# Last layer's feed-forward products by Strassen's scheme: seven products of quarters, the second product's left operands by way of DRAM

## The chip, the cores and the metric

The kernel runs on one core of a Trainium2 chip. The metric is the device time of one execution, in microseconds (us); a lower time is better.

## The reference

Three different layers follow one another on one sequence of 1024 rows with 1024 features (all float32): a hybrid layer with gated linear attention, a layer with an mLSTM and windowed attention, and a layer with a gated delta net and neighbourhood attention. The change lies in the end of the third. Its mixer's result `mix` is projected, added to x and normalized, and then comes the feed-forward part with 4096 hidden features:

```python
D_FF_3 = 4 * D_MODEL            # 4096, D_MODEL = 1024
...
mix = jnp.einsum('bte,ed->btd', jnp.concatenate([o_gdn, o_na], axis=-1), w_out[l])
x = layer_norm(DEEPNORM_ALPHA * x + mix, ln1_g[l], ln1_b[l])
ff = jnp.square(jax.nn.relu(jnp.einsum('btd,df->btf', x, w1[l]) + b1[l]))
ff = jnp.einsum('btf,fd->btd', ff, w2[l]) + b2[l]
x = layer_norm(DEEPNORM_ALPHA * x + ff, ln2_g[l], ln2_b[l])
```

## The kernel before

Engines: TensorE (PE) multiplies, VectorE (DVE), ScalarE (ACT) and GpSimd (POOL) do the elementwise work, SyncE (SP) issues the DMAs in one queue, in order. Operations are written into the program in one order per engine; each engine takes its own in order and waits at semaphores. Names of tiles come with a running number.

Every float32 operand of a product is split into a high and a low part of a shorter float32 (`fp32r`): hi is a cast by ACT, lo = x - hi a subtraction by DVE (`part`, and `piece`, L67 and L68, for weights). A product is then three matmuls, hi·hi, hi·lo and lo·hi (L123 to L125 in `tm`, L139 to L141 in `fm`). One matmul here is 128 by 128 against 512 columns.

Weights arrive in 512 KB pieces: `piece` loads into a tile `wraw` (a pool of two buffers, `rawpool`), casts, subtracts and frees it; the parts lie in `w` (six buffers). So only two such loads are under way or held at a time. The left operand x, turned so that features lie on partitions, lies in the four tiles `Thi`, `Tlo` of `new_T` (pool `tpool`, four buffers of 16 KB per partition).

The tail of the third layer has three parts:

- `out_late` finishes the output projection for eight blocks m of 128 rows: it loads the partial sum into `acc[m]`, adds two products on DVE (L335), normalizes (`ln_rows`, L248 to L255: ACT Square and Identity, DVE multiply L254, POOL add L255) and turns the rows into `T4` by eight transposes (`put_T`, L106).
- `up(g)` makes 256 hidden features of all 1024 rows: 2 halves x 2 x 8 x 3 = 96 matmuls; ACT takes Relu and Square, and a cast and a DVE subtraction split the result into `hh`, `hl` in SBUF.
- `down` multiplies them with the rows of the second weight and adds to `acc` on DVE (L1973): 8 row blocks x 2 x 2 x 3 = 96 matmuls.

With 16 groups g these are 16 x 192 = 3072 matmuls. `up(g + 1)` is written ahead of `down(g)`. At the last group the final normalization (`ln_halves`, L263 to L270) follows each row block and its two halves go out. GpSimd adds the bias b2 to each `acc[m]` once (L1962).

## Time and profile before

| what | value |
|---|---|
| three runs | 3817.88, 3821.74, 3827.13 us (median 3821.74) |
| the profiled execution's own time | 3819.98 us |
| its span in the trace | 3818.3 us |
| mean granted clock | 0.98 of full speed |

The span is what the trace covers from the first to the last instruction; the profiled execution's time lies 1.7 us above it. All times below in the rows are us from the start of the span; durations of single instructions are in ns where a view says mean ns. Matmuls are pipelined: the trace gives one about 0.39 us, but they start every 0.23 us, so their spacing and not their duration counts.

### The profile page before, as it was taken

The numbers are of one execution on the slowest core, as the hardware profiler recorded it, in microseconds if no ns is written. First come the engines' busy times: TensorE is split into PE (matmuls) and PEld (weight loads), VectorE is DVE, ScalarE is ACT, GpSimd is POOL, SyncE is SP. The second block draws the span as 40 slices with busy tenths as digits, with TensorE's granted clock in tenths as the row PEclk, the third lists the DMA queues.
The fourth block names the chain that finished last, engine by engine and source line by source line (L and its number), as shares of the span: only waits on it lengthen the run. The fifth ranks groups of instructions, "written<-read, shape, count | busy, mean of one in ns | idle before, by whom it ended". The sixth has DMA issues, their size and how long they took to land.

```text
span 3818.3 us, 49447 instructions
## 1 busy us (share of the span) xinstructions
PE 3680.5 (96%) x18856; PEld 3067.6 (80%) x18856; DVE 1901.2 (50%) x4073; ACT 1288.7 (34%) x2767; POOL 588.9 (15%) x637
## 2 busy tenths in 40 slices
...
GB/s 128 50 61 72 45 56 80 132 186 54 34 51 84 128 173 56 34 56 45 56 45 55 108 128 129 103 92 134 109 146 131 128 100 50 45 45 55 45 49 51
DMA packets 182556, 317.48 MB, mean 83 GB/s; under 512 B 33296, under 2 KB 112400, under 8 KB 182320
## 3 DMA queue, kind: packets, MB, share of 16 engines
...
q14 instruction: 87, 0.71, 0.1%
...
## 4 chain that ended last, share of the span: by engine, by line
PE 83%; DVE 8%; DMA 4%; ACT 3%; issue 1%; POOL 1%; SPq 1%; DVEq 0%; ACTq 0%; POOLq 0%
PE mm L123 11%; PE mm L125 11%; PE mm L124 11%; PE mm L139 6%; PE mm L141 6%; PE mm L140 6%; PE mx L139 4%; PE mx L141 4%; PE mx L140 4%; PE mx L123 3%; PE mx L124 3%; PE mx L125 3%; PE pt L106 1%; DVE ip L1523 1%; PE mx L1772 1%
## 5 line engine op out<-in xcount | busy, mean ns | idle before, releaser
L123 PE MATMUL mm<-w,Thi 128*128 128x512 f32 (+1 forms) x1920 | 685.5, 357 | 14.4 <-ACT Thi L111 3.1
L125 PE MATMUL mm<-w,Tlo 128*128 128x512 f32 (+1 forms) x1920 | 676.5, 353 | 0.0
L124 PE MATMUL mm<-w,Thi 128*128 128x512 f32 (+1 forms) x1920 | 674.6, 351 | 1.0 <-DVE w L68 1.0
L139 PE MATMUL mm<-Thi,w 128*128 128x512 f32 (+1 forms) x1240 | 496.6, 401 | 10.0 <-DVE qo L513 4.9
L140 PE MATMUL mm<-Tlo,w 128*128 128x512 f32 (+1 forms) x1240 | 491.1, 396 | 0.0
L141 PE MATMUL mm<-Thi,w 128*128 128x512 f32 (+1 forms) x1240 | 490.2, 396 | 0.0
L67 ACT CAST w<-wraw 128x1024 fp32r<-128x1024 f32 (+2 forms) x253 | 261.0, 1034 | 646.3 <-PE mx L125 423.5
L123 PEld LDWEIGHTS mm<-w,Thi 128*128 128x128 f32 x1920 | 365.2, 190 | 66.1 <-DVE acc L335 5.1
L125 PEld LDWEIGHTS mm<-w,Tlo 128*128 128x128 f32 x1920 | 365.0, 190 | 49.9 <-issue 3.5
L124 PEld LDWEIGHTS mm<-w,Thi 128*128 128x128 f32 x1920 | 365.4, 190 | 47.5 <-issue 2.5
L68 DVE TENSOR_TENSOR w<-wraw,w 128x1024 fp32r<-128x1024 f32 (+2 forms) x210 | 262.1, 1250 | 236.0 <-ACT w L67 230.5
L57 POOL TENSOR_TENSOR st<-st,expo 128x1 f32<-128x1 f32 x48 | 47.6, 991 | 1569.2 <-DVE st L264 1446.4
L139 PEld LDWEIGHTS mm<-Thi,w 128*128 128x128 f32 (+1 forms) x1240 | 235.0, 189 | 64.7 <-issue 9.4
L139 PE MATMUL mx<-Thi,w 128*128 128x512 f32 (+1 forms) x760 | 285.3, 375 | 0.5 <-DVE anm L1047 0.2
L140 PE MATMUL mx<-Tlo,w 128*128 128x512 f32 (+1 forms) x760 | 284.2, 374 | 0.2 <-DVE Tlo L112 0.2
L141 PE MATMUL mx<-Thi,w 128*128 128x512 f32 (+1 forms) x760 | 284.1, 374 | 0.0
L141 PEld LDWEIGHTS mm<-Thi,w 128*128 128x128 f32 (+1 forms) x1240 | 234.7, 189 | 52.6 <-issue 2.6
L140 PEld LDWEIGHTS mm<-Tlo,w 128*128 128x128 f32 (+1 forms) x1240 | 235.0, 189 | 50.4 <-issue 2.5
L123 PE MATMUL mm<-w,hh 128*128 128x512 f32 x432 | 170.9, 396 | 0.2 <-DVE acc L1208 0.2
L124 PE MATMUL mx<-w,hh 128*128 128x512 f32 x432 | 170.9, 396 | 0.0
L125 PE MATMUL mx<-w,hl 128*128 128x512 f32 x432 | 170.8, 395 | 0.0
L123 PE MATMUL mx<-w,hh 128*128 128x512 f32 x432 | 170.7, 395 | 0.0
...
## 6 DMA issues: line engine op xcount, KB each, us to landing
...
```

What stands on the lines that cost most here:

```text
L57: self.nc.gpsimd.tensor_tensor(ap, ap, self.expo[:parts, :n], op=ALU.pow)
L67: nc.scalar.copy(w[:, 1], raw)
L68: (nc.gpsimd if self.pool_lo else nc.vector).tensor_sub(w[:, 0], raw, w[:, 1].bitcast(F32))
L106: nc.tensor.transpose(pt[:, k], src[:, (j + k) * P:(j + k + 1) * P], self.idn)
L123: nc.tensor.matmul(ps, hi[:, k, cs], wh, start=start and x == 0, stop=False)
L124: nc.tensor.matmul(ps, hi[:, k, cs], wl, start=False, stop=False)
L125: nc.tensor.matmul(ps, lo[:, k, cs], wh, start=False, stop=stop and x == K - 1)
L139: nc.tensor.matmul(ps, wh, hi[:, k0 + k], start=k == 0, stop=False)
L140: nc.tensor.matmul(ps, wh, lo[:, k0 + k], start=False, stop=False)
L141: nc.tensor.matmul(ps, wl, hi[:, k0 + k], start=False, stop=k == K - 1)
L1523: nc.vector.tensor_mul(v, X[:, c0:r, c0:c0 + n].rearrange("p j c -> p c j"), row[:, None, c0:r].to_broadcast([P, n, r - c0]))
L1772: nc.tensor.matmul(ps[:, :nk], qv, kv, start=True, stop=True)
```

## The change

Both products of the feed-forward part are written as two by two quarters and done by seven products of quarters in place of eight (Winograd's form of Strassen's scheme). For the up product x has the quarters A11 to A22 (512 rows by 512 features) and each unit u of 256 hidden features has four weight quarters a, b, cc, d of 512 by 128; the sums of quarters of x are S1 to S4, those of the weights are made in place by `combine` on GpSimd. Products accumulate in PSUM and ACT copies intermediate sums aside (`snap`). For the down product the left quarters are the hidden features: their sums are made as each unit is finished (`left_parts`), and all seven left operands of each unit are written to DRAM (`hid`, 256 KB each), from where `left` loads them again, two units in one 512 KB load, and splits them into hi and lo. x itself goes to DRAM (`xs_scr`) behind the first normalization and comes back into `acc` ahead of the down product. A unit has 7 x 12 = 84 matmuls in the up product; the down product has 4 groups of four units, each with 7 products of 48 matmuls.

The diff, cut where "..." stands (the removed code of the feed-forward part is printed above):

```diff
@@ -321,11 +321,16 @@
-def out_late(c, w, scale, T, ks, y, g, b, acc, T4, junk):
+def out_late(c, w, scale, T, ks, y, g, b, acc, T4, junk=None, each=None):
     nc = c.nc
     W = [rows_of(c, w[j], ks, scale) for j in range(2)]
+    if each is not None:
+        new, acc = acc, {}
     for m in range(NT):
+        if each is not None:
+            acc[m] = new(m)
...
-        ln_rows(c, acc[m], sm, g, b, junk)
-        c.put_T(T4, m, acc[m])
+        if each is None:
+            ln_rows(c, acc[m], sm, g, b, junk)
+            c.put_T(T4, m, acc[m])
+        else:
+            jk = c.rawpool.tile([P, 2, 512], F32, name="wraw", tag="wraw")
+            ln_rows(c, acc[m], sm, g, b, jk.rearrange("p a b -> p (a b)"))
+            each(m, acc[m])
...
+LEFT = ("A11", "A12", "A22", "S1", "S2", "S3", "S4")
+OF = {1: "A11", 2: "A12", 3: "S4", 4: "A22", 5: "S1", 6: "S2", 7: "S3"}
+class Quarters:
+    def __init__(self, c, T, pool, spool):
+        self.c, self.T, self.spool = c, T, spool
+        self.S = {n: [pool.tile([P, 4, 512], F32R, name=f"{n}{x}") for x in "hl"] for n in ("S2", "S3", "S4")}
+        self.kept = {}
...
+    def put(self, n, x, src):
+        c = self.c
+        pt = c.ps_tr.tile([P, 4, P], F32, name="pt", tag="tr")
+        for k in range(4):
+            c.nc.tensor.transpose(pt[:, k], src[:, k * P:(k + 1) * P], c.idn)
+        hi, lo = self.get(n)
+        cs = slice(x * P, (x + 1) * P)
+        c.part(hi[:, :, cs], lo[:, :, cs], pt)
+    def take(self, m, x):
+        nc = self.c.nc
+        lo, hi = slice(0, 512), slice(512, D)
+        if m < 4:
+            self.kept[m] = x
+            self.put("A11", m, x[:, lo])
+            self.put("A12", m, x[:, hi])
+            return
+        y = self.kept.pop(m - 4)
+        s1, s3 = (self.spool.tile([P, 512], F32, name="s", tag="s", bufs=3) for _ in range(2))
+        nc.vector.tensor_add(s1, x[:, lo], x[:, hi])
+        nc.gpsimd.tensor_sub(s3, y[:, lo], x[:, lo])
+        nc.vector.tensor_sub(y[:, lo], s1, y[:, lo])
+        nc.vector.tensor_sub(y[:, hi], y[:, hi], y[:, lo])
+        for n, src in (("A22", x[:, hi]), ("S1", s1), ("S2", y[:, lo]), ("S3", s3), ("S4", y[:, hi])):
+            self.put(n, m - 4, src)
+def combine(nc, a, b, cc, d):
+    nc.gpsimd.tensor_sub(b, d, b)
+    nc.gpsimd.tensor_add(a, b, a)
+    yield
+    nc.gpsimd.tensor_sub(b, cc, a)
+    nc.gpsimd.tensor_sub(a, d, a)
+    yield
+def wino_up(c, src, units, Q, sink):
+    def split(raw, n):
+        w = c.wpool.tile([P, 2, 4, n], F32R, name="w", tag="w", bufs=NW)
+        nc.scalar.copy(w[:, 1], raw)
+        nc.vector.tensor_sub(w[:, 0], raw, w[:, 1].bitcast(F32))
+        return w
+    def prep(u):
+        r1, r2 = (c.rawpool.tile([P, 4, 256], F32, name="wraw", tag="wraw") for _ in range(2))
+        nc.sync.dma_start(r1, src(u)[:, 0:4])
+        nc.sync.dma_start(r2, src(u)[:, 4:8])
+        f, g = slice(0, P), slice(P, 2 * P)
+        steps = combine(nc, r1[:, :, f], r1[:, :, g], r2[:, :, f], r2[:, :, g])
+        w1 = split(r1[:, :, f], P)
+        next(steps)
+        w67 = split(r1, 2 * P)
+        next(steps)
+        w54 = split(r1, 2 * P)
+        w23 = split(r2, 2 * P)
+        return {1: (w1, f), 6: (w67, f), 7: (w67, g), 5: (w54, f), 4: (w54, g), 2: (w23, f), 3: (w23, g)}
...
+    def snap(ps):
+        t = Q.spool.tile([P, 512], F32, name="snap", tag="h")
+        nc.scalar.copy(t, ps)
+        return t
+    W = {0: prep(0)}
+    X = {0: c.mm_ps()}
+    product(1, W[0], X[0], True)
+    c11 = snap(X[0])
+    for u in range(units):
+        w, x = W.pop(u), X.pop(u)
+        if u + 1 < units:
+            W[u + 1] = prep(u + 1)
+        last = u == units - 1
+        y, z = c.mx_ps(), c.mx_ps()
+        if last:
+            product(2, w, y, True)
+        else:
+            product(5, w, z, True)
+        product(6, w, x, False)
+        u2 = snap(x)
+        if not last:
+            product(2, w, y, True)
+        C = {"C11": (y, c11)}
+        product(7, w, x, False)
+        u3 = snap(x)
+        if last:
+            product(5, w, z, True)
+        else:
+            X[u + 1] = c.mm_ps()
+            product(1, W[u + 1], X[u + 1], True)
+            c11 = snap(X[u + 1])
+        C["C22"] = (z, u3)
+        sink(u, C)
+        product(4, w, x, False)
+        C["C21"] = (x, None)
+        sink(u, C)
+        product(3, w, z, False)
+        C["C12"] = (z, u2)
+        sink(u, C)
+def wino_down(c, src, hid, groups, acc, pool, evict):
+    def left(n, u0, u1):
+        t = c.tpool.tile([P, KT, 512], F32R, name="Ahl", tag="T")
+        for u in range(u0, u1, 2):
+            k = min(2, u1 - u)
+            raw = c.rawpool.tile([P, 2, 512], F32, name="wraw", tag="wraw")[:, :k]
+            nc.sync.dma_start(raw, hid[LEFT.index(OF[n]), u:u + k].rearrange("u p n -> p u n"))
+            hi, lo = t[:, u - u0:u - u0 + k], t[:, 4 + u - u0:4 + u - u0 + k]
+            nc.scalar.copy(hi, raw)
+            nc.vector.tensor_sub(lo, raw, hi.bitcast(F32))
+        return t
+    def right(u0, u1):
+        parts = []
+        for x, u in enumerate(range(u0, u1, 2)):
+            k = min(2, u1 - u)
+            q = []
+            for n, (j, o) in (("d", (1, 1)), ("b", (1, 0)), ("a", (0, 0)), ("c", (0, 1))):
+                t = pool.tile([P, 2, 512], F32, name=f"r{n}{x}", tag=f"r{n}{x}", bufs=1)[:, :k]
+                nc.sync.dma_start(t, src[j][:, 2 * u + o:2 * (u + k):2])
+                q.append(t)
+            d, b, a, cc = q
+            parts.append((a, b, cc, d, combine(nc, a, b, cc, d)))
...
+        yield 1, split(0)
+        step()
+        yield 6, split(0)
+        yield 7, split(1)
+        step()
+        yield 4, split(1)
+        yield 5, split(0)
+        yield 3, split(3)
+        yield 2, split(2)
+    for g, (u0, u1) in enumerate(groups):
+        final = g == len(groups) - 1
+        for n, W in right(u0, u1):
+            A = left(n, u0, u1)
+            if n in (1, 5, 2):
+                ps = banks()
+            K = u1 - u0
+            row, j = {1: (0, 0), 6: (0, 1), 7: (1, 1), 4: (1, 0), 5: (1, 1), 3: (0, 1), 2: (0, 0)}[n]
+            for x in range(4):
+                cs = slice(x * P, (x + 1) * P)
+                for k, (wh, wl) in enumerate(W):
+                    ah, al = A[:, k, cs], A[:, 4 + k, cs]
+                    nc.tensor.matmul(ps[x], ah, wh, start=n in (1, 5, 2) and k == 0, stop=False, skip_group_check=True)
+                    nc.tensor.matmul(ps[x], ah, wl, start=False, stop=False, skip_group_check=True)
+                    nc.tensor.matmul(ps[x], al, wh, start=False, stop=k == K - 1, skip_group_check=True)
+                m = 4 * row + x
+                evict(g, m, j, ps[x], (m, j) not in seen, final and n in (4, 5, 3, 2))
+                seen.add((m, j))
...
+    xs_scr = c.dram.tile([NT, P, D], F32, name="xs3", tag="xs3")
+    hid = c.dram.tile([7, NFF3, P, 512], F32, name="hid3", tag="hid3")
...
+            ps_ = pool(uctx, "b3q", "right")
+            T4 = c.new_T()
+            with ExitStack() as wctx:
+                stage = pool(wctx, "b3s")
+                Q = Quarters(c, T4, ps_, stage)
+                g1 = c.bc_row(stage, rows["ln1_g_3"], tag="g1")
+                b1 = c.bc_row(stage, rows["ln1_b_3"], tag="b1")
+                def each(m, x):
+                    nc.sync.dma_start(xs_scr[m], x)
+                    Q.take(m, x)
+                run(out_late(c, i["w3_out"], ng, T3, (2, 3, 7), y_scr, g1, b1,
+                             lambda m: stage.tile([P, D], F32, name="xn", tag=f"xn{m}" if m < 4 else "xn",
+                                                  bufs=1 if m < 4 else 2), None, each=each))
...
+            Q.spool = pool(uctx, "b3h", bufs=14)
+            made = {}
...
+                    t = Q.spool.tile([P, 512], F32, name="h", tag="h")
+                    b = b1c[:, 2 * u + int(n[2]) - 1:2 * u + int(n[2])]
+                    if sb is None:
+                        nc.scalar.activation(t, ps, AF.Relu, bias=b)
+                        nc.scalar.activation(t, t, AF.Square)
+                    else:
+                        nc.vector.scalar_tensor_tensor(t, ps, b, sb, op0=ALU.add, op1=ALU.add)
+                        nc.vector.scalar_tensor_tensor(t, t, 0.0, t, op0=ALU.max, op1=ALU.mult)
+                    have[n] = t
...
+                def out(n, t):
+                    nc.sync.dma_start(hid[LEFT.index(n), u], t)
+                    have[n] = t
+                for n in ("C11", "C12", "C22"):
+                    if n in have and "A" + n[1:] not in have:
+                        out("A" + n[1:], have[n])
+                if "C21" in have and "S1" not in have:
+                    s1, s2, s3 = new(), new(), new()
+                    nc.gpsimd.tensor_add(s1, have["C21"], have["C22"])
+                    out("S1", s1)
+                    nc.gpsimd.tensor_sub(s3, have["C11"], have["C21"])
+                    out("S3", s3)
+                    nc.vector.tensor_sub(s2, s1, have["C11"])
+                    out("S2", s2)
+                if "C12" in have and "S4" not in have:
+                    s4 = new()
+                    nc.vector.tensor_sub(s4, have["C12"], have["S2"])
+                    out("S4", s4)
+            wino_up(c, lambda u: i["w3_1"][u], NFF3, Q, sink)
+        for j, ms in ((0, range(4)), (1, range(4)), (1, range(4, NT)), (0, range(4, NT))):
+            for m in ms:
+                cs = slice(j * 512, (j + 1) * 512)
+                nc.sync.dma_start(acc[m][:, cs], xs_scr[m][:, cs])
...
+        wino_down(c, i["w3_2"], hid, [(4 * g, 4 * g + 4) for g in range(4)], acc, pool(ctx, "b3r", "right"), evict)
```

The order of the instructions changes at three places that matter below. The first is SyncE's queue where `out_late` loads its rows. Before, rows of `acc` (the partial sums y3), two vectors of the normalization and the next weights (rows L329, L168 and L65; what an instruction waits for stands behind it, DMAHW being other transfers):

```order
L329 DMA acc4_25630<-y3_17838 128x1024 [waits PE_49]
L329 DMA acc5_25631<-y3_17838 128x1024
L329 DMA acc6_25632<-y3_17838 128x1024 [waits DMAHW6_49,DVE_49,PE_49]
L329 DMA acc7_25633<-y3_17838 128x1024 [waits DMAHW7_49]
L168 DMA bc_25641<-in_r_ln1_g_3 128x1024 [waits DMAHW0_49]
L168 DMA bc_25643<-in_r_ln1_b_3 128x1024 [waits DMAHW1_49]
L65 DMA wraw_26327<-in_w3_2 128x1024 [waits DMAHW2_49,DVE_49]
L65 DMA wraw_26332<-in_w3_2 128x1024 [waits DMAHW3_49,DVE_49]
L65 DMA wraw_26465<-in_w3_1 128x1024 [waits DMAHW4_49,DMAHW2_49,DVE_49]
L65 DMA wraw_26470<-in_w3_1 128x1024 [waits DMAHW5_49,DMAHW3_49,DVE_49]
```

After, at the same place (L334 loads a row block of partial sums into `xn`, L2170 stores a normalized one to DRAM, L428 and L429 are unit 0's weights):

```order
L2170 DMA xs3_25623<-xn_25774 128x1024 [waits DMAHW7_49,Pool_49]
L2170 DMA xs3_25623<-xn_25824 128x1024 [waits DMAHW0_49,Pool_49]
L2170 DMA xs3_25623<-xn_25874 128x1024 [waits DMAHW1_49,Pool_49]
L334 DMA xn_26028<-y3_17838 128x1024 [waits DMAHW1_49,DVE_49,DMAHW2_49,PE_49,Pool_49]
L2170 DMA xs3_25623<-xn_25951 128x1024 [waits DMAHW3_49,Pool_49]
L2170 DMA xs3_25623<-xn_26028 128x1024 [waits DMAHW4_49,Pool_49]
L334 DMA xn_26105<-y3_17838 128x1024 [waits DMAHW3_49,DMAHW5_49,DVE_49,PE_49]
L428 DMA wraw_26186<-in_w3_1 128x1024 [waits DMAHW6_49,Activation_49]
L429 DMA wraw_26187<-in_w3_1 128x1024 [waits DMAHW7_49,Activation_49]
L2170 DMA xs3_25623<-xn_26105 128x1024 [waits DMAHW0_49,Pool_49]
```

Block 6 (`xn_26028`) and block 7 (`xn_26105`) share two buffers with blocks 4 and 5, so their loads now wait, and block 7's load and unit 0's weights stand behind the store of block 6.

The second place is the same queue between the up and the down part. Before, weights of the two products alternate with nothing between them:

```order
L65 DMA wraw_26599<-in_w3_2 128x1024 [waits DMAHW4_49,DVE_49]
L65 DMA wraw_26604<-in_w3_2 128x1024 [waits DMAHW5_49,DVE_49]
L65 DMA wraw_26745<-in_w3_1 128x1024 [waits DMAHW2_49,DVE_49]
L65 DMA wraw_26750<-in_w3_1 128x1024 [waits DMAHW3_49,DVE_49]
L65 DMA wraw_26879<-in_w3_2 128x1024 [waits DMAHW6_49,DMAHW4_49,DVE_49]
```

After, the right operands of the first group (`ra0` to `rd1`) stand behind a load of left operands from `hid` (L510), with stores of hidden features (L2200) between them:

```order
L510 DMA wraw_28694<-hid3_25624 128x2x512 [waits DMAHW2_49,DMAHW0_49,DVE_49]
L524 DMA rd0_28458<-in_w3_2 128x2x512 [waits DMAHW1_49,PE_49]
L524 DMA rb0_28460<-in_w3_2 128x2x512
L524 DMA ra0_28462<-in_w3_2 128x2x512 [waits DMAHW3_49]
L524 DMA rc0_28464<-in_w3_2 128x2x512 [waits DMAHW4_49]
L2200 DMA hid3_25624<-h_28398 128x512 [waits DMAHW5_49,Pool_49]
L524 DMA rd1_28466<-in_w3_2 128x2x512 [waits DMAHW6_49,PE_49]
L2200 DMA hid3_25624<-h_28399 128x512 [waits DMAHW7_49,DVE_49]
L2200 DMA hid3_25624<-h_28400 128x512 [waits DMAHW0_49,Pool_49]
L524 DMA rb1_28468<-in_w3_2 128x2x512 [waits DMAHW1_49]
L2200 DMA hid3_25624<-h_28419 128x512 [waits DMAHW2_49,DVE_49]
L524 DMA ra1_28470<-in_w3_2 128x2x512 [waits DMAHW3_49]
```

The pool of `ra0` to `rd1` takes the memory of the tiles S2, S3 and S4. The reload of x (`acc0` first, L2225) follows behind one more right operand, two loads of left operands and a store.

The third is GpSimd in the middle of the up product. Before, the whole stage has eight additions of the bias there (and the small powers of the last normalizations):

```order
L57 TENSOR_TENSOR st_26023<-st_26023,expo_86 128x1 [waits DVE_49]
L255 TENSOR_TENSOR acc7_25633<-acc7_25633,bc_25643 128x1024 [waits DVE_49]
L1962 TENSOR_TENSOR acc0_25626<-acc0_25626,bc_26052 128x1024 [waits DMAHW7_49,DVE_49]
L1962 TENSOR_TENSOR acc1_25627<-acc1_25627,bc_26052 128x1024 [waits DVE_49]
L1962 TENSOR_TENSOR acc2_25628<-acc2_25628,bc_26052 128x1024 [waits DVE_49,Pool_49]
```

After, the following repeats with each unit (L407, L408, L410 and L411 are `combine` of the weights in the raw buffers, L2207 and L2209 the sums S1 and S3 of the hidden features of an earlier unit):

```order
L407 TENSOR_TENSOR wraw_27481<-wraw_27482,wraw_27481 128x4x128 [waits DMAHW4_49,DMAHW3_49,DVE_49]
L408 TENSOR_TENSOR wraw_27481<-wraw_27481 128x4x128 [waits DVE_49,Pool_49]
L2207 TENSOR_TENSOR h_27453<-h_27450,h_27433 128x512 [waits Activation_49]
L2209 TENSOR_TENSOR h_27455<-h_27430,h_27450 128x512 [waits DMAHW7_49]
L410 TENSOR_TENSOR wraw_27481<-wraw_27482,wraw_27481 128x4x128 [waits DVE_49]
L411 TENSOR_TENSOR wraw_27481<-wraw_27482,wraw_27481 128x4x128 [waits Pool_49]
L407 TENSOR_TENSOR wraw_27621<-wraw_27622,wraw_27621 128x4x128 [waits DMAHW5_49,DMAHW4_49,DVE_49]
```

Six instructions for each of 16 units stand there now, in fixed order, four of them on the two raw buffers.

## Rows read from the trace of the kernel before

**Rows 1.** The page: the span, and TensorE's busy time.

```profile
span 3818.3 us, 49447 instructions
...
PE 3680.5 (96%) x18856; PEld 3067.6 (80%) x18856; DVE 1901.2 (50%) x4073; ACT 1288.7 (34%) x2767; POOL 588.9 (15%) x637
```

**Rows 2.** Busy time (and instructions) of each engine by stretch, granted clock, DMA share, GB/s.

```profile
3049.00:3058.00 9.00, 8.02 (x31) 6.50 (x32) 3.75 (x6) 2.93 (x5) 0.00 (x0) 0.52 0.91 330
3096.00:3120.00 24.00, 21.07 (x98) 16.77 (x98) 16.79 (x19) 12.67 (x20) 9.69 (x4) 0.93 0.50 155
3120.00:3700.00 580.00, 580.00 (x2528) 475.40 (x2527) 238.30 (x314) 156.09 (x215) 20.58 (x8) 1.00 0.15 48
```

**Rows 3.** The same for TensorE alone, within the feed-forward stage.

```profile
3120.00:3780.00 660.00, 660.00 (x2877) 1.00 0.14 46
```

**Rows 4.** Timeline of TensorE and VectorE at the end: start, duration (us).

```profile
3809.03 0.40 PE L125 MATMUL mx<-w,hl 128*128 128x512 f32 x1
...
3809.47 0.69 DVE L1973 TENSOR_TENSOR acc<-acc,mx 128x512 f32<-128x512 f32 x1
3813.75 1.41 DVE L270 SCALAR_TENSOR_TENSOR acc<-acc,st,bc 128x512 f32<-128x512 f32 x2
```

**Rows 5.** Timeline of GpSimd, and the chain of waits, around out_late.

```profile
3089.69 2.39 POOL L255 TENSOR_TENSOR acc<-acc,bc 128x1024 f32<-128x1024 f32 x1 [2.94 <-DVE acc L254]
3109.07 2.35 POOL L255 TENSOR_TENSOR acc<-acc,bc 128x1024 f32<-128x1024 f32 x1 [3.48 <-DVE acc L254]
...
3074.84 0.87 PE pt L106 x8
```

**Rows 6.** Groups by line and shape, 3100 to the end: count, busy us, mean ns.

```profile
L1973 DVE TENSOR_TENSOR acc<-acc,mm 128x512 f32<-128x512 f32 x112 | 77.0, 687 | 129.6 <-PE mm L125 129.5
L68 DVE TENSOR_TENSOR w<-wraw,w 128x1024 fp32r<-128x1024 f32 x60 | 76.4, 1274 | 23.7 <-ACT w L67 23.1
L1947 DVE TENSOR_TENSOR hl<-r,hh 128x512 fp32r<-128x512 f32 x64 | 44.2, 691 | 197.8 <-ACT hh L1946 197.8
L268 DVE SCALAR_TENSOR_TENSOR acc<-acc,st,bc 128x512 f32<-128x512 f32 x16 | 11.2, 744 | 0.0
...
L67 ACT CAST w<-wraw 128x1024 fp32r<-128x1024 f32 x59 | 62.0, 1050 | 302.2 <-PE mx L125 253.5 <-PE mm L125 36.7 <-PE mx L141 10.5
L1944 ACT ACTIVATE r<-mm,b1c 128x512 f32<-128x512 f32 x32 | 22.0, 688 | 140.0 <-PE mm L141 139.8 <-DMA b1c<-in_c_b 0.2
```

**Rows 7.** The same groups for GpSimd, whole span.

```profile
L68 POOL TENSOR_TENSOR w<-wraw,w 128x1024 fp32r<-128x1024 f32 x31 | 78.3, 2530 | 41.1 <-ACT w L67 37.8 <-PE mx L141 3.3
L1748 POOL TENSOR_TENSOR nGr<-nGr,rowm 128x528 f32<-128x528 f32 x8 | 9.3, 1157 | 17.2 <-DMA nGr<-in_rpb_q 14.1 <-PE mm L125 3.1
```

**Rows 8.** Single lines of code: shortest, median and longest duration (ns).

```profile
L254 DVE TENSOR_TENSOR acc<-acc,bc x8: 1215/1226/3442, 3067.8 to 3107.8; 128x1024 f32<-128x1024 f32 x8
...
L255 POOL TENSOR_TENSOR acc<-acc,bc x8: 2350/2396/3453, 3069.4 to 3109.1; 128x1024 f32<-128x1024 f32 x8
...
L1971 DVE SCALAR_TENSOR_TENSOR acc<-acc,mm x8: 675/686/689, 3148.9 to 3172.5; 128x512 f32<-128x512 f32 x8
```

**Rows 9.** Timeline of VectorE and GpSimd where the two overlap.

```profile
3097.00 1.22 DVE L68 TENSOR_TENSOR w<-wraw,w 128x1024 fp32r<-128x1024 f32 x1
3098.13 3.44 DVE L254 TENSOR_TENSOR acc<-acc,bc 128x1024 f32<-128x1024 f32 x1
...
3097.03 3.45 POOL L255 TENSOR_TENSOR acc<-acc,bc 128x1024 f32<-128x1024 f32 x1 [3.42 <-DVE acc L254]
```

**Rows 10.** The chain of waits: start, duration of one 512 KB load.

```profile
1.24 5.41 DMA bc<-in_r_pre
...
3042.11 3.99 DMA wraw<-in_w
```

**Rows 11.** What SyncE's DMA queue waited for, 3100 to the end: us, times, longest.

```profile
SPq L65 <- DVE w L68: 594.1, 57, 21.4
```

131 lines of the change are left out of this document (72 added, 59 removed).

## The prediction

> **What bounds the kernel now.** I read the page first. TensorE is busy for 96% of the span [rows 1], so only fewer matmuls or less idle time of TensorE can shorten it. Then the table by stretch: from 3120 to 3700, in the feed-forward stage, TensorE is busy without a gap at the full granted clock, DVE for 41% of the time, ACT for 27%, POOL for 4%, and the DMA engines move 48 GB/s at a share of 0.15 [rows 2]. The stage is bound by TensorE alone. The only large wait in it is that of SyncE's queue for free raw buffers, 594.1 us [rows 11]; it costs nothing, since TensorE never waits.
>
> The price of a matmul is its spacing: 2877 of them in 660 us are 0.2294 us each [rows 3]. All 3072 take 704.7 us. The last starts at 3809.03 [rows 4], so the stage runs as if it had begun, without a gap, at 3809.3 - 704.7 = 3104.6.
>
> **What goes.** 16 units x 84 and 28 products x 48 matmuls are 2 x 1344 = 2688, that is 384 fewer: 384 x 0.2294 = **-88.1 us**. Shapes are the same (128 by 128 against 512), so I take the same spacing. Evictions into `acc` fall from 256 to 112, but DVE was not the bound, so that gains nothing.
>
> **Before the first product: +31.4 us.** The sums S1 to S4 of x need rows of both halves (m and m - 4), and product 5 of unit 0, the second to be done, needs S1 of all of blocks 4 to 7. Before, the first products followed as soon as one half was turned; the last block's addition began at 3109.07 [rows 5]. Now blocks 6 and 7 wait for a buffer. Block 4's addition ends at 3092.1 [rows 5]. Its tile is free when its store has landed; no store of this size stands in the rows, so I take a load of 512 KB, 4.0 to 5.4 us [rows 10], at the lower end as the queue is otherwise idle. Block 6's load lands 4 us later, at 3100. One normalization is two DVE adds of 0.69, two ACT passes of 1024 elements (1.05 each [rows 6], here with a sum, say 1.2), DVE's multiply 1.23 and POOL's add 2.4 [rows 8], and some 2 us of short operations: 9.4 us, so block 6 is done at 3109.5. On SyncE, block 7's load stands behind the store of block 6: issued at 3110, landed at 3114, normalized at 3123.5. POOL's first weight sums (2.5 us) get ahead of its addition: 3126. Then three DVE sums, and 20 transposes in place of 8 (0.87 for eight [rows 5]) with a cast and a subtraction for each four: 7.5 us, 3133.5. TensorE has then done 13 matmuls, 3 us. Unit 1's weights can't be loaded before unit 0's buffers are free, so another stall of some 5.5 us follows. As if begun at 3133.5 - 3 + 5.5 = 3136, against 3104.6: +31.4. Bounds: 24 (no second stall, short stores) and 40 (each of the two transfers and the two normalizations 2 us longer). The half clock after an idle stretch is in it: from 3049 to 3058, after a longer wait, the granted clock was 0.52 [rows 2], the lower level, which costs up to 4 us once.
>
> **The up product: +8 us.** TensorE needs 84 x 0.2294 = 19.3 us for a unit. The two raw buffers are held through a unit's whole chain of weight sums: load (4.0 [rows 10]); POOL's L407 and L408; cast and subtraction of the first pair; POOL's S1 and S3, which stand between in its order; L410 and L411; two casts and two subtractions. POOL has no 512-element sum in the rows; 528 elements took 1.16 us and 1024 took 2.39 to 2.53 [rows 7, 8], so I take 1.2, with 1.1 and 2.4 as ends. Casts of 1024 are 1.05, subtractions 1.27 [rows 6]. The chain: 4.0 + 0.7 (subtraction of the first quarter, between the two sums) + 2.4 + 1.05 + 1.27 + 2.4 x 1/2 (half of S1 and S3 beside the cast) + 2.4 + 1.05 + 1.27 + 1.27 = 16.6; DVE's sums S2, S4 and C12 stand between them (0.69 each [rows 6], some 1.5 in the way), and some twelve hand-offs from engine to engine take 1 to 1.5: 19.1 to 19.6. DVE and POOL exclude one another: POOL's add of 2.4 took 3.45 beside DVE's subtraction of 1.22, and DVE's multiply behind it 3.44 in place of 1.22 [rows 8, 9]; an operation with one operand in PSUM was never stretched (675 to 689 ns [rows 8]). In a unit DVE has four weight subtractions, three squares and two sums, 8.0 us of two SBUF operands, and POOL 7.2: 15.2 of 19.3 us exclude one another. I put some 0.4 us of blocking on the chain for that, an estimate between none and the 2.2 of [rows 9]. I take 19.8 per unit: 0.5 x 16 = +8. Bounds: 0, and 40 with 1 us more at each POOL pair.
>
> The Trainium skill (SBUF — State Buffer, section "SBUF: two separate sides") says that a DVE operation with two SBUF inputs and a GpSimd operation that reads SBUF take an exclusive lock, and that whichever comes second blocks for the whole of the first. The trace agrees (3.44 and 3.45 us where they overlapped). Without the lock the loop would be 19.4 us, up +2 and the sum 3790; by the lock it is as summed here. The rule speaks against putting the sums on POOL.
>
> Stores of hidden features (29.4 MB) and weight loads are 7 x 256 + 1024 KB in 19.8 us, some 145 GB/s; in the stretch at 3049 the queue moved 330 [rows 2]. They are hidden; ACT has 7 us of work in a unit.
>
> **Between up and down: +17 us.** Before, `up` and `down` alternate, so nothing is empty. Now the left operands of product 7 take T's second half, which product 4 of the last unit frees 12 matmuls before the end of up, E; the load behind it, which stands ahead of the right operands on SyncE, is issued at about E. TensorE's product 1 needs `ra0` and `ra1`: the left load, seven right loads and four stores are 5.2 MB, at the 330 GB/s of [rows 2] 15.8 us; then one cast, 1.05, less 1.4 for the six matmuls that start with `ra0`. With the lower clock after such an idle time (some 2 us lost) 17. Bounds: 11 (a third of it moved before E) and 26 (half the rate for half of it).
>
> **The down product: +2 us.** A product is 48 x 0.2294 = 11.0 us. DVE has four subtractions of 1.27 and four evictions of 0.69: 7.8. The reload from DRAM cycles two raw buffers: 4.0 + 1.05 + 1.27 = 6.3 us each [rows 6, 10], one per product. POOL's eight sums of 2.53 lie in 77 us. All hidden, and weights and left operands are ahead by up to three products. 0 to 28 (1 us each).
>
> **The tail: +6 us.** Before, 9.3 us lie between the last matmul's start and the end [rows 1, 4]. Now all final normalizations fall into the last three products, 33 us: 12 evictions, 16 statistics of the same width and 32 passes of 0.744 [rows 6] are 43 us of DVE, from E - 30 to E + 13, then the store: 15.5. Bounds 2 and 9.
>
> **Sum.** -88.1 + 31.4 + 8 + 17 + 2 + 6 = -23.7. The profiled execution took 3819.98 us: 3796.3. The median of the runs, 3821.74, is 1.8 above it; I take **3797**.
>
> **Rivals.**
> - *The weight chain bounds the up product* (slower). If each POOL sum waits for a DVE subtraction in full, the loop is 21.5 to 22.5 us: 16 x (2.2 to 3.2) = 35 to 51 in place of 8, 3824 to 3840. It decides from 21.3 us on, where the whole gain is gone. For it: 15.2 of 19.3 us exclusive, POOL's fixed order, both stretched rows [rows 9]. Against: TensorE sets the pace of the hidden sums, so they fall at the same place each time.
> - *Nearly the full gain*: stores land soon and the queues run ahead; prologue 24, up 0, transition 11, tail 3: -50, 3770 (3762 to 3784). For it: 594 us of slack in the queue before [rows 11], which shows that loads are early when buffers are there. Against: here they are not.
> - *The reload from DRAM bounds the down product*: 12.5 us per product for 11.0, 28 x 1.5 = 42, 3836. Against: 6.3 of 11 us for a buffer. For it: loads stand behind those of right operands, whose tiles are single.
>
> **How the numbers follow.** My forecast (3784 to 3812) 0.50, the weight chain 0.22 (3812 to 3842), nearly the full gain 0.17, the down product 0.08, something else 0.03. About 0.2%, 7.6 us, is what a measurement of this kernel can tell from no change. Faster by more: 0.50 + 0.17 + 0.04 from the weight chain's lower end and the rest = 0.71; within 0.11; slower 0.18. The range 3768 to 3832 leaves some 0.05 below and 0.13 above.
>
> **What will show it.** In the profile after, TensorE's units should start every 19.8 us in the up product, with short waits for `w`; a spacing over 21 is the first rival. Its waits before unit 0's product 5 and unit 1's should add up to some 30 us, one wait of 12 to 18 us should stand between up and down, and the last matmul should lie some 15 us from the end. L407 to L411 should take 1.2 us where DVE is idle and 2.0 to 2.5 where not. I am wrong if the matmuls are spaced otherwise than 0.23, or if the stores hold back the loads.

## The result, and the profile after the change

The kernel after the change takes 3801.84 us (median of four runs, 3798.97 to 3803.52), the kernel before 3824.43 in the four runs taken beside it: a ratio of 0.9942, with a 95% interval of 0.9925 to 0.9959. It is faster by 22.6 us, and the forecast of 3797 is 4.8 us below. The profiled execution took 3798.97, with a span of 3797.2 against 3818.3 [rows 1].

The head of the page after, with the busy time, share and instructions of each engine:

```profile
span 3797.2 us, 49400 instructions
PE 3624.9 (95%) x18520; PEld 3017.2 (79%) x18520; DVE 2075.1 (55%) x4145; ACT 1329.6 (35%) x2779; POOL 830.8 (22%) x769
```

To see where the 21.1 us between the spans lie, I split the last stage at fixed instructions. It begins with the first transposes of `no` in the mixer's last part (L1907 before, L2141 after). A term is the time that a part took, less 0.2294 us for each of its matmuls: *start* is the part to the start of the 85th matmul of the up product, *up* its rest, *between* reaches from there to the start of the 49th matmul of the down product, *down* is the rest of it, *tail* what follows the last matmul. A wait ahead of the 85th or the 49th matmul so counts to the part before it. All times in us; the kernel before has no such parts within, and one of its own for the start (to the 3104.6 of the forecast) and the tail.

| | forecast (change) | before | after | change |
|---|---|---|---|---|
| matmuls x 0.2294 | -88.1 | 704.7 | 616.6 | -88.1 |
| start | +31.4 | 55.1 | 89.9 | +34.8 |
| up | +8 | 0 | 4.7 | +4.7 |
| between | +17 | 0 | 11.9 | +11.9 |
| down | +2 | 0 | 3.5 | +3.5 |
| tail | +6 | 9.0 | 12.7 | +3.7 |
| the stage | -23.7 | 768.9 | 739.3 | -29.5 |
| ahead of the stage | 0 | 3049.4 | 3057.9 | +8.4 |

The last row was in no term of the forecast. In the mixer, ahead of all that the change touches, the same instructions run in the same order, and the kernel after still falls behind. The table by stretch of both kernels, PEclk being the granted clock as a share of full speed; first the kernel before, then the one after:

```profile
2760.00:2780.00 20.00, 19.11 (x136) 15.64 (x134) 15.92 (x59) 11.09 (x40) 9.74 (x15) 1.00 0.29 90
```
```profile
2740.00:2760.00 20.00, 17.42 (x100) 14.27 (x98) 13.67 (x54) 8.49 (x34) 8.03 (x12) 0.83 0.42 135
2760.00:2780.00 20.00, 19.55 (x72) 15.54 (x73) 10.47 (x39) 5.57 (x19) 6.10 (x9) 0.51 0.12 35
```

TensorE is busy in both, but at 0.51, the lower level of 1.2 GHz, it starts 72 instructions in 20 us in place of 136. In the executions profiled below the stage begins anywhere from 3047.1 to 3063.1, whatever was changed in it. The loss belongs to the execution at least as much as to the kernel: 33 executions of the unchanged kernel before, taken beside the experiments, lie between 3811.78 us (mean granted clock 0.982) and 3833.98 (0.974), the slower ones at the lower clock; the four of the kernel after all have 0.970 or 0.971. The clock differs within the stage too: in its first 10 us, whose code the change leaves alone, it was anywhere from 0.58 to 0.81 in the executions profiled. So kernels are compared here by the length of the stage as well as by the median of their runs, and starts that lie 2 to 4 us apart tell nothing.

The largest waits of TensorE from 3090 on in the kernel after, by the line that waits and what it waits for (us in all, times, longest):

```profile
PE mm L567 <- ACT w L535: 8.4, 2, 8.2
PE pt L381 <- DVE Tlo L112: 5.5, 3, 3.1
PE mx L567 <- DVE acc L2239: 4.4, 3, 3.9
PE pt L381 <- DVE S3l L112: 4.0, 1, 4.0
PE pt L381 <- DVE S2l L112: 3.9, 2, 2.0
PE mm L123 <- DVE xn L340: 3.8, 1, 3.8
```

L567 is a matmul of the down product: it waits once for its first right operand (8.2) and once for DVE (3.9). L381 are the transposes of the sums of x: their waits belong to the start. No wait of the up product in its steady units is among them. Its pace is read from the first matmul with S2 of two units that lie ten apart, in the timeline of TensorE (start, duration):

```profile
3227.97 0.40 PE L445 MATMUL mm<-S2h,w 128*128 128x512 f32 x1
...
3421.57 0.40 PE L445 MATMUL mm<-S2h,w 128*128 128x512 f32 x1
```

193.6 us for ten units are 19.36 each, 84 x 0.2305: TensorE alone sets the pace.

**The start.** SyncE's queue in the kernel after (start, duration, which includes a wait where several are grouped):

```profile
3101.19 0.32 SPq L334 DMA_DIRECT2D xn<-y  x1
3105.50 9.74 SPq L2170 DMA_DIRECT2D xs<-xn  x2
3118.33 0.32 SPq L334 DMA_DIRECT2D xn<-y  x1
```

Block 6 is loaded at 3101.2 and block 7 only at 3118.3. In SyncE's queue its load stands behind block 6's store, which leaves at 3114.9, as soon as GpSimd has ended block 6's addition (L255). Then it waits 3.1 us more for the tile of block 5, and the last to read that are the transposes of block 5's right half on TensorE, which stand behind those of block 4's sums. GpSimd adds block 7 only at 3132.5, behind unit 0's first weight sums:

```profile
3112.54 2.35 POOL L255 TENSOR_TENSOR xn<-xn,bc 128x1024 f32<-128x1024 f32 x1 [2.95 <-DVE xn L254]
...
3132.49 2.38 POOL L255 TENSOR_TENSOR xn<-xn,bc 128x1024 f32<-128x1024 f32 x1
```

TensorE's transposes of block 7 wait 4.0 us for DVE, and product 5 of unit 0 starts at 3142.4:

```profile
3138.37 0.63 PE L381 MATMUL pt<-idn,xn 128*128 128x128 f32 x4 [4.04 <-DVE S3l L112]
...
3142.40 1.39 PE L445 MATMUL mx<-Thi,w 128*128 128x512 f32 x2
```

**Between up and down.** The timeline of SyncE, then those of ACT and TensorE:

```profile
3460.23 0.37 SPq L510 DMA_DIRECT2D wraw<-hid  x1
...
3461.68 0.46 SPq L524 DMA_DIRECT2D ra<-in_w  x1
```
```profile
3468.03 1.04 ACT L535 CAST w<-ra 128x1024 fp32r<-128x1024 f32 x1 [3.18 <-DMA ra<-in_w]
```
```profile
3469.13 1.22 PE L567 MATMUL mm<-w,Ahl 128*128 128x512 f32 x2 [8.24 <-ACT w L535]
...
3473.14 0.63 PE L568 MATMUL mm<-w,Ahl 128*128 128x512 f32 x1
3473.56 0.50 PE L569 MATMUL mm<-w,Ahl 128*128 128x512 f32 x1
3473.90 0.39 PE L567 MATMUL mm<-w,Ahl 128*128 128x512 f32 x1
```

The load of the first right operand leaves at 3461.7, as the up product ends (3460.7), lands some 6 us later and is cast. The first matmuls behind the gap are 0.43 apart, and from 3473.9 on 0.23: the clock comes back (0.50 from 3465 to 3470, 1.00 from 3475 on). The first 24 matmuls need `ra0` alone; `ra1` is cast at 3476.1, and the 25th matmul waits 0.2 us for it.

**The down product.** Its one larger wait is for an eviction on DVE. The timeline of the engines ahead of it:

```profile
3548.51 10.01 POOL L2234 TENSOR_TENSOR acc<-acc,bc 128x1024 f32<-128x1024 f32 x3 [4.62 <-DVE acc L2239]
3556.20 3.41 DVE L513 TENSOR_TENSOR Ahl<-wraw,Ahl 128x1024 fp32r<-128x1024 f32 x1
3560.13 2.81 DVE L513 TENSOR_TENSOR Ahl<-wraw,Ahl 128x1024 fp32r<-128x1024 f32 x1
3561.82 3.37 POOL L2234 TENSOR_TENSOR acc<-acc,bc 128x1024 f32<-128x1024 f32 x1
3565.15 3.38 POOL L410 TENSOR_TENSOR rb<-rc,ra 128x1024 f32<-128x1024 f32 x1
3568.56 1.05 ACT L535 CAST w<-rb 128x1024 fp32r<-128x1024 f32 x1 [5.62 <-POOL rb L410]
3569.65 2.34 DVE L536 TENSOR_TENSOR w<-rb,w 128x1024 fp32r<-128x1024 f32 x1 [2.78 <-ACT w L535]
3571.91 3.36 DVE L513 TENSOR_TENSOR Ahl<-wraw,Ahl 128x1024 fp32r<-128x1024 f32 x1
3575.20 0.67 DVE L2239 TENSOR_TENSOR acc<-acc,mx 128x512 f32<-128x512 f32 x1
3576.02 0.63 PE L567 MATMUL mx<-w,Ahl 128*128 128x512 f32 x1 [3.95 <-DVE acc L2239]
```

L2234 adds the bias b2 to `acc`, eight times. In GpSimd's order the eight stand between the weight sums of the same group (L408, L410), within 42 us. Beside them DVE's subtractions L513 take 2.81 to 3.41 us in place of 1.27 [rows 6]. But DVE was idle for 2.8 us just ahead of the wait: the weight sum L410 had come late, behind the last addition, ACT's cast waited for it and DVE's subtraction L536 for the cast. That subtraction and L513 then stood ahead of the eviction (0.67, one operand in PSUM). Behind the wait nine matmuls are 0.43 us apart, which costs another 1.8.

### The profile page after: what moved, and what is told of

It is laid out like the page before. It is cut to its first block, busy times and chain, and to the rows that moved or that the text cites. A ratio compares the mean times of both kernels' runs of the same rounds, so it can differ in the third digit from the quotient of the medians.

```text
span 3797.2 us, 49400 instructions
## 1 busy us (share of the span) xinstructions
PE 3624.9 (95%) x18520; PEld 3017.2 (79%) x18520; DVE 2075.1 (55%) x4145; ACT 1329.6 (35%) x2779; POOL 830.8 (22%) x769
## 5 line engine op out<-in xcount | busy, mean ns | idle before, releaser
L139 PE MATMUL mm<-Thi,w 128*128 128x512 f32 (+1 forms) x984 | 395.8, 403 | 8.6 <-DVE qo L747 4.4
L140 PE MATMUL mm<-Tlo,w 128*128 128x512 f32 (+1 forms) x984 | 390.7, 397 | 0.0
L141 PE MATMUL mm<-Thi,w 128*128 128x512 f32 (+1 forms) x984 | 390.0, 397 | 0.0
L67 ACT CAST w<-wraw 128x1024 fp32r<-128x1024 f32 (+1 forms) x189 | 193.7, 1028 | 342.0 <-PE mx L125 169.9
L68 DVE TENSOR_TENSOR w<-wraw,w 128x1024 fp32r<-128x1024 f32 (+1 forms) x146 | 180.8, 1241 | 209.1 <-ACT w L67 204.5
L139 PEld LDWEIGHTS mm<-Thi,w 128*128 128x128 f32 (+1 forms) x984 | 186.6, 190 | 52.9 <-issue 8.9
L141 PEld LDWEIGHTS mm<-Thi,w 128*128 128x128 f32 (+1 forms) x984 | 186.2, 189 | 42.5 <-issue 2.6
L139 PE MATMUL mx<-Thi,w 128*128 128x512 f32 (+1 forms) x504 | 185.1, 367 | 0.5 <-DVE anm L1281 0.2
L140 PE MATMUL mx<-Tlo,w 128*128 128x512 f32 (+1 forms) x504 | 184.2, 365 | 0.2 <-DVE Tlo L112 0.2
L141 PE MATMUL mx<-Thi,w 128*128 128x512 f32 (+1 forms) x504 | 183.9, 365 | 0.0
L112 DVE TENSOR_TENSOR Tlo<-pt,Thi 128x512 fp32r<-128x512 f32 (+2 forms) x144 | 91.8, 655 | 100.6 <-ACT Thi L111 99.8
L68 POOL TENSOR_TENSOR w<-wraw,w 128x1024 fp32r<-128x1024 f32 (+1 forms) x43 | 108.2, 2522 | 99.1 <-ACT w L67 97.3
L111 ACT CAST Thi<-pt 128x512 fp32r<-128x512 f32 (+2 forms) x144 | 77.5, 564 | 148.4 <-PE pt L106 107.8
```

The costliest lines, as they stand in the source:

```text
L67: nc.scalar.copy(w[:, 1], raw)
L68: (nc.gpsimd if self.pool_lo else nc.vector).tensor_sub(w[:, 0], raw, w[:, 1].bitcast(F32))
L111: self.nc.scalar.copy(hi, src)
L112: self.nc.vector.tensor_sub(lo, src, hi.bitcast(F32))
L139: nc.tensor.matmul(ps, wh, hi[:, k0 + k], start=k == 0, stop=False)
L140: nc.tensor.matmul(ps, wh, lo[:, k0 + k], start=False, stop=False)
```

## The experiments

The parts of the stage in each run, as in the table above (us). "Stage" goes from the same transposes to the end of the span.

| run | start | up | between | down | tail | stage |
|---|---|---|---|---|---|---|
| after the change | 89.9 | 4.7 | 11.9 | 3.5 | 12.7 | 739.3 |
| 1 late rows in own tiles | 82.4 | 2.5 | 12.4 | 3.3 | 12.8 | 729.8 |
| 2 down alone | 59.3 | -4.0 | -0.1 | 11.4 | 12.7 | 740.1 |
| 3 two more sums | 89.9 | 30.2 | 12.0 | 3.3 | 12.7 | 764.7 |
| 4 bias spread | 88.6 | 2.5 | 11.9 | -3.4 | 12.8 | 729.0 |
| 5 1 + 4 + right operands early | 82.2 | 2.5 | 20.2 | -1.0 | 12.9 | 733.4 |
| 6 5 + square elsewhere | 84.5 | 2.8 | 19.9 | -0.6 | 12.9 | 736.2 |
| 7 6 + product 2 first | 81.7 | 2.5 | 19.3 | -1.0 | 12.9 | 732.1 |
| 8 2 + 4 | 63.0 | -4.0 | -0.1 | 1.2 | 12.7 | 733.5 |
| 9 1 + 4 | 83.1 | 2.5 | 11.2 | -2.9 | 12.7 | 723.4 |
| 10 9 + both loads early | 81.9 | 8.4 | 18.7 | -0.2 | 12.9 | 738.4 |

A term can be below zero, since in parts of the products matmuls are 0.2264 to 0.229 us apart. Runs 2 and 8 have 2880 matmuls, the others 2688.

**Experiment 1: rows of the late blocks in tiles of their own.** Is the start bound by the loads of blocks 6 and 7, as the forecast had it?

```diff
-   lambda m: stage.tile([P, D], F32, name="xn", tag=f"xn{m}" if m < 4 else "xn", bufs=1 if m < 4 else 2)
+def row_tile(m):
+    if m < 6:
+        return stage.tile([P, D], F32, name="xn", tag=f"xn{m}", bufs=1)
+    if not late:
+        late.append(c.wpool.tile([P, 2, D], F32, name="w", tag="w", bufs=NW))
+    return late[0][:, m - 6]
```

> Blocks 6 and 7 get buffers of their own (one of the six weight buffers), so their loads no longer wait for blocks 4 and 5. My theory (the 43 us lost ahead of the first products are mostly the queue of late row blocks: two buffers, freed only when the block's sums are turned): block 7's load leaves before 3065 in place of 3118, product 5 of unit 0 starts 12 to 18 us earlier than 3142, and the time falls by as much, to about 3787. Rival: the normalizations, transposes and subtractions on VectorE, ScalarE and GpSimd are the limit whatever the loads do: under 5 us earlier, 3797 or more.

Measured: 3779.17 (3768.63 to 3782.59, five runs), ratio to before 0.9874 [0.9852, 0.9897]. The start falls by 7.5 us. The wait for the tile was real, but behind it stands another bound. The table by stretch of this run (busy us of TensorE, its loads, DVE, ACT and POOL; clock; DMA share; GB/s):

```profile
3090.00:3120.00 30.00, 19.10 (x85) 14.36 (x83) 29.21 (x44) 14.39 (x24) 17.64 (x12) 0.76 0.29 106
```

DVE is busy for 29.2 of 30 us; in the kernel after it was 20.7 of 30 in the stretch that lies as far behind the stage's first transposes. With the rows there in time, the sums, the normalization and the subtractions of the low parts follow one another on DVE with hardly a break, and TensorE's waits are for DVE's results. Some 8.3 us of that time are six operations that GpSimd's work made longer; the same sum of two operands in SBUF, undisturbed and not, and then the start of product 5:

```profile
3101.14 0.67 DVE L397 TENSOR_TENSOR s<-xn 128x512 f32<-128x512 f32 x1
...
3112.04 2.49 DVE L397 TENSOR_TENSOR s<-w 128x512 f32<-128x512 f32 x1
```
```profile
3133.51 1.05 PE L445 MATMUL mx<-Thi,w 128*128 128x512 f32 x2
```

The 12 to 18 us that were expected for product 5 did not come: counted from the stage's first transposes it starts after 82.5 us, 2.1 earlier than in the kernel after (84.5). The other 5.5 us of the 7.5 lie behind it, where unit 1's weights, loaded 8.1 us earlier, are there in time. That DVE, and its collisions with GpSimd, hold the rest is read from the busy time; no run took work off DVE. Of the 22.7 us between the medians (3801.84 and 3779.17) the stage accounts for 9.5.

**Experiment 2: the down product alone.** The up product is plain again (96 matmuls a unit, from `T4`), `acc` stays in SBUF, the hidden features and the Strassen form of the down product are as in the change.

```diff
-Q = Quarters(c, T4, ps_, stage)
-run(out_late(..., each=each))
+run(out_late(c, i["w3_out"], ng, T3, (2, 3, 7), y_scr, g1, b1, acc, T4, stage.tile([P, D], F32, name="junk")))
...
-wino_up(c, lambda u: i["w3_1"][u], NFF3, Q, sink)
+for u in range(NFF3):
+    W = c.slab(i["w3_1"][u], n=256, kp=4)
+    for r, f in ((0, 0), (1, 1), (1, 0), (0, 1)):
+        ps = c.any_ps()
+        c.fm(T4, W, r, ps, f * P, P)
+        ...
```

> Only the down product has seven products; the up product is the old one (1536 matmuls), x stays in SBUF, and the right operands of the first group have memory of their own. My theory (the up half is worth nothing net: 44 us fewer matmuls against some 43 lost ahead of it and 5 in it): no stall ahead of up, a smaller one between up and down since x is not reloaded; 3784 to 3797, as fast as the whole change or faster. Rival: the loss ahead of the first products has another cause than the sums of quarters of x, and stays: 3835 or more.

Measured: 3791.79 (3786.61 to 3795.33, six runs), 0.9917 [0.9899, 0.9935]. With half of the saving (192 matmuls, 44.0 us) the stage is as long as with the whole: 740.1 against 739.3. The start is nearly that of before (59.3 against 55.1), and the gap between the products is gone: here the right operands lie in memory that nothing held before, and x is not reloaded (the run doesn't tell the two apart). So the start and the gap are the price of the up half: (89.9 - 59.3) + 12 = 42.6 of its 44.0 us, or 38.9 with the start of experiment 8 (63.0), which has the same code there and a lower clock in its first 10 us. Without the gap, the down product loses more, 11.4, of it 9.3 in waits for evictions into `acc`.

**Experiment 3: two idle sums more on GpSimd in each unit.** How near is the chain of weight sums to the bound? Two sums with results that nobody reads are added.

```diff
     yield
+    if more is not None:
+        nc.gpsimd.tensor_sub(more, cc, a)
+        nc.gpsimd.tensor_sub(more, d, a)
     nc.gpsimd.tensor_sub(b, cc, a)
...
```

> The whole change, with two idle GpSimd sums of 512 elements (2.6 us) added to each unit of the up product between the first and the second pair. By the trace GpSimd waits 1.7 us per unit at that place and TensorE sets the pace of 19.36 us, so the chain of the raw buffers takes about 17.7 us: with 2.6 more it is 20.3, some 14 us in all over 15 units. By the forecast's sum (19.8 for the chain) the period becomes 22.4, 45 us in all. If the chain is far off the path, nothing changes.

Measured (one execution): 3816.63; up grows from 4.7 to 30.2. The first matmuls with S2 of two units that lie nine apart:

```profile
3251.72 0.40 PE L448 MATMUL mm<-S2h,w 128*128 128x512 f32 x1
...
3438.67 0.40 PE L448 MATMUL mm<-S2h,w 128*128 128x512 f32 x1
```

A unit takes 186.95/9 = 20.77 us. Now the chain binds, and TensorE waits for `w`. The two added sums (L411 and L412 of this run: count, busy us, mean ns), and a wait that GpSimd still had in each unit of the kernel after:

```profile
L412 POOL TENSOR_TENSOR more<-wraw 128x512 f32<-128x512 f32 x11 | 23.3, 2115 | 0.8
L411 POOL TENSOR_TENSOR more<-wraw 128x512 f32<-128x512 f32 x11 | 14.7, 1339 | 0.8
```
```profile
3308.56 1.80 POOL L2207 TENSOR_TENSOR h<-h 128x512 f32<-128x512 f32 x1 [1.69 <-ACT h L2190]
```

Less the added sums, 1.34 and 2.12, the chain of the change is 17.3 us; by the wait of 1.7 for hidden features, which TensorE paces, it is 17.7. Both are estimates, and put the chain 1.7 to 2.1 us under TensorE's 19.36. The forecast's loop of 19.8 was so 2.1 to 2.5 us too long; but two sums are enough to make the chain the bound.

**Experiment 4: the bias additions spread.** One addition every four evictions over the second and third group, in place of eight at the start of the second.

```diff
+        calls, turn = [0], (4, 5, 0, 1, 2, 6, 7, None, None, 3)
...
-                for x in range(NT):
+            calls[0] += g >= 1
+            if g >= 1 and calls[0] % 4 == 1 and calls[0] // 4 < len(turn):
+                x = turn[calls[0] // 4]
+                if x is not None:
                     nc.gpsimd.tensor_add(acc[x], acc[x], rb["b2_3"])
```

> The whole change, with GpSimd's eight bias additions written one at a time behind the products of groups 1 and 2 instead of all at the start of group 1. My theory (the 4.3 us gap of TensorE at 3571 is VectorE's subtractions and GpSimd's additions blocking one another while the additions and the weight sums come together): the gap is gone and nothing else changes, 3 to 4 us less, 3794. Rival: the gap comes from the weight sums alone, and stays at 4 us.

Measured (one execution): 3784.75, stage 729.0. The wait of 3.9 us for `acc` is gone, and the down product falls from 3.5 to -3.4, by 6.9: the wait, 0.8 in shorter ones and the matmuls at the lower clock behind them make up most of it. One wait of 0.3 us for DVE is left in it. Single additions still took 3.12 us in the mean (3.24 before), so they still meet DVE's subtractions; but the weight sums are no longer held up: the first L410 of the second group starts 81.2 us behind the first matmul of the down product, not 89.4. Of the 10.3 us that the stage fell, 2.2 lie in the up product, which the edit doesn't touch.

**Experiment 5: 1 and 4, and the first group's right operands from GpSimd's queue**, so that their loads need not stand behind the last unit's on SyncE.

```diff
-nc.sync.dma_start(t, src[j][:, 2 * u + o:2 * (u + k):2])
+(nc.gpsimd if u0 == 0 else nc.sync).dma_start(t, src[j][:, 2 * u + o:2 * (u + k):2])
```

> The whole change with three repairs: own buffers for row blocks 6 and 7, the bias additions spread, and the eight loads of the first group's right operands issued from GpSimd's queue, where they wait for nothing but the memory of S2 and S3 (free 11 and 8 us before the end of up). My theory (the 11.9 us lost between up and down are those loads, 4.2 MB that leave only at the end of up because they stand behind a load of left operands): TensorE's gap of 8.6 us falls under 3 us, 8 to 10 us less in that stage, and the time is near 3765. Rival: the reload of x and the left operands keep the DMA engines full anyway, and product 6 waits for its weight sums: 3 us or less gained there, 3772.

Measured: 3782.39 (3776.09 to 3793.54, five runs), 0.9897 [0.988, 0.9914]; the gap grew from 8.4 to 13.7, and a second wait, 3.8 us for an eviction ahead of the 49th matmul, brings the part to 20.2. The gain did not come, but the edit did only half of what it was to do. Of the eight loads the first four left before the end of the up product (3440.1), and `ra0` landed at 3443.7; the last four waited for the last product with S4 and left behind it. The timeline of POOL:

```profile
3434.03 0.94 POOL L524 DMA_DIRECT2D rd<-in_w  x1 [7.48 <-PE mm L447]
...
3440.52 0.72 POOL L524 DMA_DIRECT2D rd<-in_w  x1 [3.36 <-PE mx L447]
```

The DMA engines now moved 390 to 410 GB/s when the left operands of product 7 were asked for (the second load at 3440.7), and that load took 11 us to land. ACT's order has its cast ahead of that of `ra0`. The timeline of ACT, then of TensorE:

```profile
3447.82 1.04 ACT L512 CAST Ahl<-wraw 128x1024 fp32r<-128x1024 f32 x1 [7.34 <-DMA wraw<-hid]
3451.71 1.04 ACT L512 CAST Ahl<-wraw 128x1024 fp32r<-128x1024 f32 x1 [2.85 <-DMA wraw<-hid]
3452.66 1.99 ACT L535 CAST w<-ra 128x1024 fp32r<-128x1024 f32 x2
```
```profile
3453.76 1.22 PE L567 MATMUL mm<-w,Ahl 128*128 128x512 f32 x2 [13.54 <-ACT w L535]
```

The wait is named for `w`, but what came last was the load of `hid` ahead of it on ACT. `ra1` landed at 3451.9, no earlier than that load.

**Experiments 6 and 7: two guesses at the start.** Experiment 6 adds to 5 that the square of the first normalization goes to a tile of its own in place of a raw buffer (two `s` buffers in place of three make room); 7 adds that unit 0 does product 2 before product 5, which needs S1 of all rows.

```diff
-jk = c.rawpool.tile([P, 2, 512], F32, name="wraw", tag="wraw")
-ln_rows(c, acc[m], sm, g, b, jk.rearrange("p a b -> p (a b)"))
+ln_rows(c, acc[m], sm, g, b, junk)
```
```diff
-        if last:
+        if last or u == 0:
             product(2, w, y, True)
...
```

> As the run with three repairs, and the first normalization's squares go to a small tile of their own, not into the raw buffers, so that unit 0's weights are loaded before the row blocks are done. If unit 0's and 1's weights are a part of what holds the first products, the stage from the third layer's last head to the 84th matmul gets 3 to 6 us shorter. If the sums, casts and subtractions of the row blocks are all of it, nothing changes.

> As the run before in this list, and unit 0 takes product 2 (A12, of blocks 0 to 3 alone) ahead of product 6 and 5, so that TensorE has two products to do while the late blocks are made. My theory: up to 2.8 us less ahead of the first products (one product more done in idle time). Rival: TensorE waits for the transposes that stand ahead of product 2 in its order, and nothing is gained.

Measured: 3784.69 (3778.87 to 3791.59, six runs) and 3782.98 (3776.06 to 3793.2, five), 0.99 [0.9883, 0.9916] and 0.9896 [0.9878, 0.9913]; starts of 84.5 and 81.7 against 82.2 in 5. In 6 unit 0's weights are there early, and the start is no shorter, so they don't bound it. 7 differs from 6 only in the order, has 36 matmuls done in place of 24 before the last rows are ready, and its start is 2.8 us shorter, as its theory said; that makes up for what 6 had lost. Each is one execution, and starts of one and the same code lie between 81.9 and 83.1 (1, 5, 9 and 10). What is left, DVE's work, is again read from its busy time (43.4 of 50 us from 3090 to 3140 in 6) and not shown by an edit.

**Experiment 8: the down product alone, bias spread** (2 with the edit of 4).

> Only the down product has seven products, with the bias additions spread. The gaps of 2.3 and 4.0 us in its second group go away: 5 to 7 us less than the run with the down product alone, 3785 to 3787; the whole change repaired stays ahead of it by about 20 us, since its up half is then worth some 17 us net.

Measured: 3788.22 (3780.36 to 3797.71, four runs), 0.991 [0.9891, 0.9928]; down falls from 11.4 to 1.2. The additions cost more here than in 4 (10.2 against 6.9). One wait of 2.8 us for an eviction is left. The stage falls by 6.6 only, since the start was 3.7 longer with the same code.

**Experiment 9: 1 and 4 together.**

> The two repairs that each moved one wait, together: the rows of blocks 6 and 7 in tiles of their own, and the bias additions one per four evictions over the second and third group. Theory (each wait has its own cause): the gains add. From the first transposes of the late head's last part to the end of the span 739.3 us after the change, less 7.5 (rows) and less 6.9 to 10 (bias): 722 to 725 us, time 3770 to 3776 if the part before the stage takes as long as in the others (3047 to 3054 us). Rival (the gains overlap, since an earlier down product finds its weights later, or the gap between up and down grows): stage 728 or more, time 3779 or above, no better than the rows alone.

Measured: 3777.51 (3772.55 to 3783.29, five runs), 0.9885 [0.9866, 0.9904]; stage 723.4. The two gains add up: the start is 6.8 us shorter than after the change, the down product 6.4, and the up product 2.2, as in 1 and in 4. In the stage it is the shortest of all, 10.1 us below experiment 8: that is what the up half is worth once both are repaired, half of the 20 that were expected there. In the medians it can't be told from experiment 1 (0.9874), whose stage is 6.4 us longer; what comes ahead of the stage varies by more than that.

**Experiment 10: 9, with both loads early.** As in 5 the right operands come by GpSimd's queue, and product 7's left operands of the first group get raw tiles of their own.

```diff
+own = u0 == 0 and n in (7,)
-raw = c.rawpool.tile([P, 2, 512], F32, name="wraw", tag="wraw")[:, :k]
+raw = (pool.tile([P, 2, 512], F32, name="lraw", tag="lraw", bufs=2) if own else
+       c.rawpool.tile([P, 2, 512], F32, name="wraw", tag="wraw"))[:, :k]
```

> As the run before, and the first group's right operands from GpSimd's queue, and product 7's left operands of the first group by way of raw tiles of their own, so that neither load waits for raw buffers of the up product. Theory (in the run with early right operands the load of the left operands, issued last, met a full queue and held the gap at 13.7 us): with both issued some 10 us before the up product's end the gap falls from 8.4 us to 2 to 5, the stage to 716 to 720 us. Rival (the gap is bytes: stores of the last unit, left and right operands together, and the queue moves no more than some 390 GB/s): the gap stays at 8 us or more, stage 722 or more.

Measured: 3790.29 (3786.57 to 3803.36, six runs), 0.9916 [0.9898, 0.9934]; gap 16.0. The edit did not bring what it was to bring: neither load was early. The timelines of SyncE and of POOL, around the end of the up product at 3461.7:

```profile
3461.66 0.37 SPq L512 DMA_DIRECT2D lraw<-hid  x1
```
```profile
3460.64 1.29 POOL L2216 TENSOR_TENSOR h<-h 128x512 f32<-128x512 f32 x1 [11.85 <-ACT h L2199]
3461.88 1.26 POOL L2218 TENSOR_TENSOR h<-h 128x512 f32<-128x512 f32 x1
3463.09 0.94 POOL L526 DMA_DIRECT2D rd<-in_w  x1
```

The loads on GpSimd now stand behind the sums of the last unit, which wait for its last activation, and the new raw tiles came free only as the last products ended. So this run tests neither theory. It shows the price of a full queue once more: the right operands took 8.8 to 12.6 us to land (medians). The up product grew too, from 2.5 to 8.4; why was not looked into. Whether the gap can be closed at all, with both loads issued early, stays open.

## Why the prediction was right, point by point

- **What goes** (-88.1). Right: 2688 matmuls, and in the steady units 0.2305 us apart (0.2294 assumed).
- **Before the first product** (+31.4, measured +34.8, within its bounds of 24 to 40). The chain up to product 5 was right. On the clock of the kernel before (less the 8.4 us of the mixer) block 6's addition ended at 3106.5 (forecast 3109.5), block 7's load left at 3109.9 (3110), its addition ended at 3126.5 (3126) and product 5 began at 3134.0 (3133.5). One step of it was luck: behind block 6's store the load waited 3.1 us more for block 5's tile, which the forecast didn't name, and block 6 was early by as much. Too small was the loss behind the start of product 5: 8.1 us in place of 5.5, in waits (0.4, 1.0, 0.5 and 0.7), in matmuls 0.43 us apart at the lower clock and in block 7's last transposes. With the loads early (experiment 1) only 7.5 us come back, 5.5 of them from this loss; that DVE is then busy almost throughout is a bound that the forecast didn't name.
- **The up product** (+8, measured +4.7). The term was mis-sized. The chain of weight sums is some 17.3 to 17.7 us (experiment 3), not 19.8, so TensorE sets the pace; of the 4.7, some 1.4 are the spacing (19.36 for 19.27, 16 times), and most of the rest lies in the last unit, with two waits for `w` (0.9 and 0.7) that experiments 1 and 4 don't have. The blocking of DVE and POOL is there, but smaller: L410 and L411 took 1.74 and 1.62 us where L407 and L408 took 1.29 alone. The forecast said 2.0 to 2.5 and 1.2.
- **Between up and down** (+17, measured +11.9). The mechanism was right, the term mis-sized. The forecast let the first matmul wait for 5.2 MB and had six matmuls start with `ra0`. It waits for the first right operand alone, the fourth of the loads that leave as the up product ends, which landed after some 6 us, and 24 matmuls need no other; the rest of the loads came in while TensorE worked. Of the 11.9, 8.2 are the wait, and most of the rest the matmuls at the lower clock.
- **The down product** (+2, measured +3.5; -3.4 with the bias spread). Evictions were hidden, as said, except where eight bias additions stood among the weight sums of one group on GpSimd. The forecast left these out of its sum; they held up a weight sum, and two subtractions of DVE then met ahead of one eviction.
- **The tail** (+6, measured +3.7). The last matmul starts 13.0 us before the end, the forecast said 15.5.
- **The rivals.** The weight chain as bound did not come; it is 1.7 to 2.1 us per unit away, and experiment 3 shows that it would have come with two more sums. The reload bound nothing: no wait of TensorE in the down product is for left operands. Nearly the full gain came only with the repair of experiment 1 (3777.51 to 3782.98 in 1, 5, 7 and 9), and by other means than the rival had: its term for the start (24) was reached in no run with both halves (81.7 - 55.1 = 26.6 at best), that for the gap (11) nearly (11.2).

The terms behind the start came out 17 - 11.9 + 8 - 4.7 + 6 - 3.7 = 10.7 us shorter, start and down 4.9 longer, so the stage fell by 29.5 in place of 23.7. The 8.4 us in the mixer took that back: the forecast was near the result partly because two errors cancelled. That the clock fell there is shown; why, in code that the change doesn't touch, isn't settled, and the kernel before varies by as much from one execution to the next.

The rule in the Trainium skill (SBUF — State Buffer, section "SBUF: two separate sides") on the exclusive lock of DVE and GpSimd agrees in kind: POOL's additions of 2.4 us took 3.37 beside DVE's subtractions, and these 2.81 to 3.41 in place of 1.27. The added time, 1.0 on the one and 1.5 to 2.1 on the other, is less than the whole duration of the other's operation; the rows don't show how much of that had already run.
